# Feed-forward with 512-column products: the whole inner width first, then the down projection by output tile

## The chip, the cores and the metric

The kernel runs on one core of a Trainium2 chip. The metric is the device time of one execution in microseconds (us); smaller is better. The kernel before takes 1467.88 us as a median of three runs.

## The reference, cut to what matters

A network of two blocks works on 256 tokens of width 1024. The first block is two mixing layers with attention (called "even" and "odd" in the kernel). The second has two layers, each a feed-forward, a mixing stage, and another feed-forward; a norm ends it. The change lies in the feed-forward, which therefore runs four times (fa0, fb0, fa1, fb1):

```python
x = x + 0.5 * swiglu(rms_norm(x, norm), w_gate, w_up, w_down)
```

`swiglu(h)` is `(silu(h @ w_gate) * (h @ w_up)) @ w_down`, with an inner width of 2816, all in float32.

## The kernel before, in words

Activations lie with features on the 128 partitions and the 256 tokens along the free axis, so `x` is 8 tiles of 128 x 256. To keep float32 accuracy with the one-pass type float32r, every operand is split in a high part (rounded to float32r) and a low part (what the rounding left). A product of weight tile `w` and activation `h` is then three matmuls (`mm3`, L131 to L133): w-high with h-high, w-high with h-low, w-low with h-high, each with 256 columns, all added in one PSUM tile. The 128 x 128 weight tile is the stationary operand and is loaded anew for every matmul.

Weights come as one stream. `fetch_to` loads pieces of 128 x 1024 (512 KB) on SP's DMA queue, and for each ScalarE casts the high part (`whi`, L117) and VectorE subtracts (`wlo`, L118). There are 4 raw buffers and 5 of `whi` and `wlo`; `weight` asks for the piece 4 places ahead, so a new piece takes the buffers of the piece that TensorE has just left.

The feed-forward before (`ffn`): `scaled` makes high and low parts of `x` times the norm's gain (two separate tiles per feature tile, `hh` and `hl`). The inner width is 22 tiles. For inner tile m, `gate_up` accumulates gate and up in the two halves of one PSUM bank (2 x 8 x 3 = 48 matmuls), and `swish` multiplies by the token's norm factor straight from PSUM (L257, 512 wide), applies silu on ScalarE (L259), multiplies gate and up (L260), and splits the result (L139, L140). `down(m)` then adds this tile's part of all 8 output tiles in 4 PSUM banks (24 matmuls), two inner tiles behind the gate and up products. After the last, L242 adds half of each sum to `x`. The norm's factor comes from `squares`, `rms_sum` (L207), 12 small VectorE instructions (L185 to L191), and `rms_spread` (transposes, L199) in the middle of inner tile 2.

A scheduler of the framework puts each engine's instructions in one fixed order when the program is built; at run time each engine works through its own list and waits where an input is not there.

Of the kernel before, what the change touches and what calls it, by code (L numbers as in the profile page):

```python
# [9 lines left out]
F32 = mybir.dt.float32  # L10
# [3 lines left out]
OP = mybir.AluOpType  # L14
# [37 lines left out]
class Net:  # L52
# [90 lines left out]
    def scaled(self, gain):  # L143

        nc, ring = self.nc, self.ring
        self.h = []
        for k in range(KT):
            x = self.x[k]
            hi = ring.tile([128, S], F32R, tag=f"hh{k}", name=f"hh{k}")
            lo = ring.tile([128, S], F32R, tag=f"hl{k}", name=f"hl{k}")  # L150
            g = self.gain0[:, k:k + 1] if gain == "norm0" else self.v(gain, k)
            nc.scalar.activation(hi, x, AF.Copy, scale=g)
            nc.vector.scalar_tensor_tensor(lo, x, g, hi.bitcast(F32), op0=OP.mult, op1=OP.subtract)
            self.h.append((hi, lo))

    def squares(self):

# [63 lines left out]
    def half_silu(self, out, t):  # L221

        self.nc.scalar.activation(out, t, AF.Tanh)
        self.nc.vector.scalar_tensor_tensor(out, out, 1.0, t, op0=OP.add, op1=OP.mult)

    def ffn(self, tag, gain):
        nc, tc = self.nc, self.tc
        with ExitStack() as c:
            psum = self.banks.using(gu=(2, 0, 1), ss=(3,), acc0=(4,), acc1=(5,), acc2=(6,), acc3=(7,))
            work = c.enter_context(tc.tile_pool(name="fw", bufs=1))  # L230
            self.scaled(gain)
            acc = [psum.tile([128, 2, S], F32, tag=f"acc{i}", name=f"acc{i}") for i in range(4)]
            mid = {}

            def down(m):
                mh, ml = mid.pop(m)
                for i in range(KT):
                    self.mm3(acc[i // 2][:, i % 2], *self.weight((tag, "d", m), i * 128), mh, ml,
                             start=(m == 0 and i % 2 == 0), stop=(m == MT - 1))
                    if m == MT - 1 and i % 2 == 1:  # L240
                        for j in (i - 1, i):
                            nc.vector.scalar_tensor_tensor(self.x[j], acc[i // 2][:, j % 2], 0.5, self.x[j],  # L242
                                                           op0=OP.mult, op1=OP.add)

            def gate_up(m):
                ps = psum.tile([128, 2, S], F32, tag="gu", name="gu")
                if m == 1:
                    self.squares()
                if m == 2:
                    self.rms_sum(psum)  # L250
                self.feature_tiles(ps, (tag, "gu", m), first=m == 0,
                                   mid=(lambda: self.rms_spread(psum)) if m == 2 else None)
                return ps

            def swish(m, ps):
                t = work.tile([128, 2, S], F32, tag="t", name="t", bufs=2)
                nc.vector.tensor_tensor(t, ps, self.rsb, op=OP.mult)  # L257
                g = work.tile([128, S], F32, tag="g", name="g", bufs=2)
                nc.scalar.activation(g, t[:, 0], AF.Silu)  # L259
                nc.vector.tensor_tensor(g, g, t[:, 1], op=OP.mult)  # L260
                mid[m] = self.split(work, g, "m", bufs=4)

            ps = [gate_up(m) for m in range(3)]
            for m in range(3):
                swish(m, ps[m])
            down(0)
            for m in range(3, MT):
                swish(m, gate_up(m))
                down(m - 2)
            down(MT - 2)  # L270
            down(MT - 1)

    def feature_tiles(self, ps, key, first=False, mid=None):

# [61 lines left out]
    def ysplit(self, src_fn, k):  # L336

        nc, ring = self.nc, self.ring
        hi = ring.tile([128, S], F32R, tag=f"hh{k}", name=f"yh{k}")
        lo = ring.tile([128, S], F32R, tag=f"hl{k}", name=f"yl{k}")  # L340
        src = src_fn
        nc.scalar.copy(hi, src)
        nc.vector.tensor_tensor(lo, src, hi.bitcast(F32), op=OP.subtract)
        self.y[k] = (hi, lo)
# [894 lines left out]
    def final(self, gain, out):  # L1239
# [4 lines left out]
        o = [self.ring.tile([128, 4, S], F32, tag="raw", name="o", bufs=RAW) for _ in range(2)]  # L1244
        ps = psum.tile([128, 2], F32, tag="sum", name="sum")
        for k in range(KT):
            t = self.ring.tile([128, S], F32, tag=f"hl{k}", name="t")
# [28 lines left out]
def _cols(w, i, n=128):  # L1276
    return w[:, i * n:(i + 1) * n]
# [7 lines left out]


def _ffn(add, tag, gate, up, down):
    for m in range(MT + 2):
        if m < MT:
            add((tag, "gu", m), _t(_cols(gate, m), _cols(up, m)))  # L1290
        if m >= 2:
            add((tag, "d", m - 2), _n(down[(m - 2) * 128:(m - 1) * 128]))


HEADS = [h for t in range(4) for h in (t, 4 + t)]
# [222 lines left out]
```

## Time and profile before

| | us |
|---|---|
| median of 3 runs (1467.38 to 1471.15) | 1467.88 |
| the profiled execution | 1467.17 |
| its span on the core | 1465.4 |
| TensorE busy with matmuls | 1432.1 (98%) |
| VectorE busy | 1013.0 (69%) |
| ScalarE busy | 739.8 (50%) |
| mean granted TensorE clock | 0.991 of full speed |

The profile shows one execution. PE is TensorE's matmuls, PEld its weight loads, DVE is VectorE, ACT is ScalarE, SP issues the DMAs. Matmuls are pipelined: the duration of one overlaps the next, so what one costs is read from start to start in a timeline, not from its duration. The other 1.8 us of the profiled execution lie outside the span.

### The profile page before, as it was taken

The page shows a single profiled execution, that of the slowest core. Times are in us where ns is not written, and L with a number is a line of the kernel's source. Part 1 is how long each engine was busy: PE and PEld are TensorE (multiplying, and loading weights), DVE is VectorE, ACT ScalarE, POOL GpSimd, SP SyncE. Part 2 cuts the span into 40 slices and gives each one's busy share as a digit, 9 for nine tenths or more (in the row PEclk, how much of TensorE's full clock was granted, in tenths as well). Part 3 has the DMA queues.
Part 4 walks back from the last instruction along what each step waited for, and adds up shares of the span by engine and source line. Part 5 has one row for each costly group of instructions (what it writes and reads, how often), then busy time and mean ns, then how long its engine had stood idle before and what let it go on. Part 6 is the DMA issues. An engine that isn't in the chain of part 4 may idle for free.

```text
span 1465.4 us, 31747 instructions
## 1 busy us (share of the span) xinstructions
PE 1432.1 (98%) x13326; PEld 1370.9 (94%) x13326; DVE 1013.0 (69%) x1804; ACT 739.8 (50%) x1268; POOL 23.9 (2%) x54
## 2 busy tenths in 40 slices
PE   8899989999999999999999999999999999999997
PEld 7699979899999989898999999999998988999997
DVE  7879798886555678657655668556678756765564
ACT  6947555855444474335444445444457324544443
POOL 0000000000000000000000000000000001000000
PEclk9999999999999999999999999999999999999998
DMA  8244534265555534124555555555553213555551
GB/s 297 76 130 132 179 125 144 87 206 177 186 184 184 180 116 129 47 87 122 180 181 182 187 187 173 184 178 187 187 173 116 74 32 101 173 178 183 186 187 44
DMA packets 63600, 222.01 MB, mean 151 GB/s; under 512 B 7744, under 2 KB 9024, under 8 KB 63456
## 3 DMA queue, kind: packets, MB, share of 16 engines
q1 hardware_dynamic: 62928, 219.31, 47.0%
q8 instruction: 104, 1.70, 0.5%
q10 hardware_dynamic: 432, 0.53, 0.1%
q14 instruction: 40, 0.33, 0.1%
q0 software_dynamic: 96, 0.13, 0.0%
HBM read 218.90 MB, written 1.05 MB: 150 GB/s over the span
## 4 chain that ended last, share of the span: by engine, by line
PE 91%; ACT 4%; DVE 3%; issue 1%; POOL 1%; DMA 0%; POOLq 0%; DVEq 0%; ACTq 0%
PE gu L131 11%; PE gu L133 11%; PE gu L132 11%; PE mm L132 6%; PE mm L131 6%; PE mm L133 6%; PE acc L131 6%; PE acc L132 6%; PE acc L133 6%; PE t L975 2%; PE dx L975 1%; PE gram L992 1%; PE gu L282 1%; PE s L370 1%; ACT whi L117 1%
## 5 line engine op out<-in xcount | busy, mean ns | idle before, releaser
L118 DVE TENSOR_TENSOR wlo<-raw,whi 128x1024 fp32r<-128x1024 f32 (+1 forms) x412 | 499.1, 1213 | 209.2 <-ACT whi L117 208.8
L117 ACT CAST whi<-raw 128x1024 fp32r<-128x1024 f32 (+1 forms) x412 | 426.8, 1039 | 416.8 <-PE gu L132 167.4
L131 PE MATMUL gu<-hh,whi 128*128 128x256 f32 x1344 | 380.7, 283 | 0.1
L132 PE MATMUL gu<-hl,whi 128*128 128x256 f32 x1344 | 380.3, 283 | 0.0
L133 PE MATMUL gu<-hh,wlo 128*128 128x256 f32 x1344 | 380.2, 283 | 0.0
L131 PEld LDWEIGHTS gu<-hh,whi 128*128 128x128 f32 x1344 | 257.3, 191 | 0.6 <-issue 0.2
L133 PEld LDWEIGHTS gu<-hh,wlo 128*128 128x128 f32 x1344 | 257.4, 192 | 0.0
L132 PEld LDWEIGHTS gu<-hl,whi 128*128 128x128 f32 x1344 | 257.3, 191 | 0.0
L132 PE MATMUL acc<-ml,whi 128*128 128x256 f32 x704 | 197.6, 281 | 0.0
L133 PE MATMUL acc<-mh,wlo 128*128 128x256 f32 x704 | 197.5, 281 | 0.0
L131 PE MATMUL acc<-mh,whi 128*128 128x256 f32 x704 | 196.9, 282 | 0.1
L131 PE MATMUL mm<-hh,whi 128*128 128x256 f32 x608 | 178.4, 293 | 6.8 <-ACT whi L117 6.5
L132 PE MATMUL mm<-hl,whi 128*128 128x256 f32 x608 | 175.8, 289 | 0.1
L133 PE MATMUL mm<-hh,wlo 128*128 128x256 f32 x608 | 175.6, 289 | 0.0
L132 PEld LDWEIGHTS acc<-ml,whi 128*128 128x128 f32 x704 | 132.7, 189 | 0.0
L131 PEld LDWEIGHTS acc<-mh,whi 128*128 128x128 f32 x704 | 132.0, 189 | 0.7 <-ACT mh L139 0.3
L133 PEld LDWEIGHTS acc<-mh,wlo 128*128 128x128 f32 x704 | 132.5, 188 | 0.0
L131 PEld LDWEIGHTS mm<-hh,whi 128*128 128x128 f32 x608 | 117.1, 193 | 11.3 <-ACT whi L117 6.5
L132 PEld LDWEIGHTS mm<-hl,whi 128*128 128x128 f32 x608 | 117.2, 193 | 2.9 <-issue 1.2
L133 PEld LDWEIGHTS mm<-hh,wlo 128*128 128x128 f32 x608 | 117.0, 192 | 2.2 <-issue 0.9
L257 DVE TENSOR_TENSOR t<-gu,rs 128x512 f32<-128x512 f32 x88 | 60.4, 690 | 54.8 <-PE gu L133 54.8
L139 ACT CAST mh<-g 128x256 fp32r<-128x256 f32 x88 | 35.3, 406 | 100.4 <-DVE g L260 100.4
(396 smaller groups left out, 2210.2 us busy)
## 6 DMA issues: line engine op xcount, KB each, us to landing
raw<-in_stream SPq DMA_DIRECT2D x404, 512.0 KB, 3.5
raw<-in_stream SPq DMA_DIRECT2D x4, 280.0 KB, 2.6
x<-in_x SPq DMA_DIRECT2D x4, 256.0 KB, 5.0
raw<-in_stream SPq DMA_DIRECT2D x4, 256.0 KB, 5.2
lora<-in_lora SPq DMA_DIRECT2D x2, 512.0 KB, 5.1
dec<-in_dec SPq DMA_DIRECT2D x1, 512.0 KB, 5.5
out<-o SPq DMA_DIRECT2D x2, 256.0 KB, 3.0
out<-o ACTq DMA_DIRECT2D x2, 256.0 KB, 2.8
```

Of the source, the lines that this page charges most:

```text
L117: nc.scalar.copy(hi, raw)
L118: nc.vector.tensor_tensor(lo, raw, hi.bitcast(F32), op=OP.subtract)
L131: mm(out, ah, bh, start=start, stop=False, skip_group_check=True)
L132: mm(out, ah, bl, start=False, stop=False, skip_group_check=True)
L133: mm(out, al, bh, start=False, stop=stop, skip_group_check=True)
L139: nc.scalar.copy(hi, src)
L257: nc.vector.tensor_tensor(t, ps, self.rsb, op=OP.mult)
L282: mm(ps[:, u], part, self.h[k][0], start=(i + j == 0), stop=False, skip_group_check=True)
L370: nc.tensor.matmul(ps[:, 0:256], q[p, 128:256], kT[p, :], start=True, stop=True)
L975: nc.tensor.matmul(ps[p, n], lhs(e, p, n), rhs(e, p, n), start=True, stop=True)
L992: nc.tensor.matmul(ps[p, n], bk[p, 4 * u + n, w], ar[p, 4 * u + n], start=True, stop=True)
```

## The change

- `mmw` replaces `mm3` in the feed-forward. High and low part of an activation lie side by side in one tile, and one matmul of 512 columns multiplies w-high with both; its two results go to the two halves of a PSUM bank. A second matmul of 256 columns adds w-low with the high part to the first half. Three matmuls become two; the columns are the same.
- Gate and up now take a bank each, and whoever reads a result must add the two halves: ScalarE copies the second half out of PSUM, VectorE adds the first.
- The whole inner width comes first (22 tiles of gate and up, all results kept in SBUF), then `down` output tile by output tile, 22 products each, each followed by its own copy, add, factor and add to `x`. The norm's factor is multiplied into the gate before silu, and into the output at the end instead of into `up`.
- The weight stream is laid out in that order; the pieces keep their size and number.

```diff
     def scaled(self, gain):
...
-            hi = ring.tile([128, S], F32R, tag=f"hh{k}", name=f"hh{k}")
-            lo = ring.tile([128, S], F32R, tag=f"hl{k}", name=f"hl{k}")
+            t = ring.tile([128, 2, S], F32R, tag=f"h{k}", name=f"h{k}")
+            hi, lo = t[:, 0], t[:, 1]
...
+            self.hw.append(t.rearrange("p a t -> p (a t)"))
...
+    def mmw(self, out, ah, al, b, start, stop):
+
+        mm = self.nc.tensor.matmul
+        mm(out.rearrange("p a t -> p (a t)"), ah, b, start=start, stop=False, skip_group_check=True)
+        mm(out[:, 0], al, b[:, 0:S], start=False, stop=stop, skip_group_check=True)
...
-            psum = self.banks.using(gu=(2, 0, 1), ss=(3,), acc0=(4,), acc1=(5,), acc2=(6,), acc3=(7,))
+            psum = self.banks.using(gu=(0, 1, 2, 3, 4, 5), ss=(6,), dn=(7, 6, 2, 3))
...
             def swish(m, ps):
-                t = work.tile([128, 2, S], F32, tag="t", name="t", bufs=2)
-                nc.vector.tensor_tensor(t, ps, self.rsb, op=OP.mult)
-                g = work.tile([128, S], F32, tag="g", name="g", bufs=2)
-                nc.scalar.activation(g, t[:, 0], AF.Silu)
-                nc.vector.tensor_tensor(g, g, t[:, 1], op=OP.mult)
-                mid[m] = self.split(work, g, "m", bufs=4)
+
+                g = work.tile([128, 2, S], F32, tag="g", name="g", bufs=3)
+                for u in range(2):
+                    nc.scalar.copy(g[:, u], ps[u][:, 1])
+                    nc.vector.tensor_tensor(g[:, u], ps[u][:, 0], g[:, u], op=OP.add)
+                    if u == 0:
+                        nc.vector.tensor_tensor(g[:, 0], g[:, 0], self.rs, op=OP.mult)
+                        nc.scalar.activation(g[:, 0], g[:, 0], AF.Silu)
+                nc.vector.tensor_tensor(g[:, 0], g[:, 0], g[:, 1], op=OP.mult)
+                t = work.tile([128, 2, S], F32R, tag=f"m{m}", name="m")
+                nc.scalar.copy(t[:, 0], g[:, 0])
+                nc.vector.tensor_tensor(t[:, 1], g[:, 0], t[:, 0].bitcast(F32), op=OP.subtract)
+                mid.append(t.rearrange("p a t -> p (a t)"))
...
-            down(0)
             for m in range(3, MT):
                 swish(m, gate_up(m))
-                down(m - 2)
-            down(MT - 2)
-            down(MT - 1)
+            for i in range(KT):
+                acc = psum.tile([128, 2, S], F32, tag="dn", name="acc")
+                for m in range(MT):
+                    self.mmw(acc, *self.weight((tag, "d"), (i * MT + m) * 128), mid[m], m == 0, m == MT - 1)
+                t = work.tile([128, S], F32, tag="t", name="t", bufs=2)
+                nc.scalar.copy(t, acc[:, 1])
+                nc.vector.tensor_tensor(t, acc[:, 0], t, op=OP.add)
+                nc.vector.tensor_tensor(t, t, self.rs2[:, 0], op=OP.mult)
+                nc.vector.tensor_tensor(self.x[i], self.x[i], t, op=OP.add)
...
+    for m in range(MT):
+        add((tag, "gu", m), _t(_cols(gate, m), _cols(up, m)))
+    add((tag, "d"), down.reshape(MT, 128, KT, 128).transpose(1, 2, 0, 3).reshape(128, -1))
```

TensorE, second feed-forward, where down and gate/up products meet. Before they alternate every 48 and 24 rows (`hh`, `hl`: parts of `x`; `mh`, `ml`: parts of an inner tile):

```order
L133 MATMUL acc3_11091<-mh_11326,wlo_11285 128x256
L131 MATMUL gu_11469<-hh0_11056,whi_11341 128x256
L132 MATMUL gu_11469<-hl0_11057,whi_11341 128x256
L133 MATMUL gu_11469<-hh0_11056,wlo_11342 128x256
L131 MATMUL gu_11469<-hh1_11060,whi_11341 128x256
L132 MATMUL gu_11469<-hl1_11061,whi_11341 128x256
```

With the change the last gate/up product is followed by the first of output tile 0 (`m` is an inner tile with both parts):

```order
L230 MATMUL gu_11400<-h6_10158,whi_11311 128x512
L231 MATMUL gu_11400<-h6_10158,wlo_11312 128x256
L230 MATMUL gu_11400<-h7_10161,whi_11311 128x512
L231 MATMUL gu_11400<-h7_10161,wlo_11312 128x256
L230 MATMUL acc_11456<-m_10347,whi_11346 128x512
L231 MATMUL acc_11456<-m_10347,wlo_11347 128x256
L230 MATMUL acc_11456<-m_10358,whi_11346 128x512
L231 MATMUL acc_11456<-m_10358,wlo_11347 128x256
```

Each group of three rows is now two, and the down rows stand together behind all 22 inner tiles.

VectorE, one inner tile of the same feed-forward. Before:

```order
L257 TENSOR_TENSOR t_11831<-gu_11770,rs_11279 128x512
L118 TENSOR_TENSOR wlo_11843<-raw_11840,whi_11842 128x1024
L260 TENSOR_TENSOR g_11833<-g_11833,t_11831 128x256
L140 TENSOR_TENSOR ml_11837<-g_11833,mh_11836 128x256
L118 TENSOR_TENSOR wlo_11874<-raw_11871,whi_11873 128x1024
L118 TENSOR_TENSOR wlo_11904<-raw_11901,whi_11903 128x1024
```

With the change, VectorE and then ScalarE, the same inner tile (L262 copies the second half, L263 adds the first):

```order
L263 TENSOR_TENSOR g_11331<-gu_11285,g_11331 128x256
L265 TENSOR_TENSOR g_11331<-g_11331,rs_10314 128x256
L118 TENSOR_TENSOR wlo_11347<-raw_11344,whi_11346 128x1024
L263 TENSOR_TENSOR g_11331<-gu_11286,g_11331 128x256
L267 TENSOR_TENSOR g_11331<-g_11331 128x256
L118 TENSOR_TENSOR wlo_11369<-raw_11366,whi_11368 128x1024
L270 TENSOR_TENSOR m_11339<-g_11331,m_11339 128x256
```

```order
L262 COPY g_11331<-gu_11285 128x256
L117 CAST whi_11346<-raw_11344 128x1024
L266 ACTIVATE g_11331<-g_11331 128x256
L262 COPY g_11331<-gu_11286 128x256
L117 CAST whi_11368<-raw_11366 128x1024
L269 CAST m_11339<-g_11331 128x256
```

Per inner tile there are now two weight pieces instead of three, and five small VectorE rows instead of one of 512 columns and two of 256; ScalarE has four small rows instead of two, with a weight cast behind each of the two copies.

TensorE, first mixing stage, up to the spread that waits for ScalarE's `wide`. Before, the head sums (L912) stand 16 rows ahead of it:

```order
L131 MATMUL mm_7184<-hh2_6427,whi_6704 128x256
L132 MATMUL mm_7184<-hl2_6428,whi_6704 128x256
L133 MATMUL mm_7184<-hh2_6427,wlo_6705 128x256
L131 MATMUL mm_7184<-hh3_6431,whi_6704 128x256
L132 MATMUL mm_7184<-hl3_6432,whi_6704 128x256
L133 MATMUL mm_7184<-hh3_6431,wlo_6705 128x256
L131 MATMUL mm_7184<-hh4_6435,whi_6704 128x256
L903 MATMUL spread_6815<-ident_74,wide_6813 128x128 x4
```

With the change they stand 12 rows ahead of it:

```order
L131 MATMUL mm_6710<-h0_5953,whi_6230 128x256
L132 MATMUL mm_6710<-h0_5953,whi_6230 128x256
L133 MATMUL mm_6710<-h0_5953,wlo_6231 128x256
L131 MATMUL mm_6710<-h1_5956,whi_6230 128x256
L132 MATMUL mm_6710<-h1_5956,whi_6230 128x256
L133 MATMUL mm_6710<-h1_5956,wlo_6231 128x256
L131 MATMUL mm_6710<-h2_5959,whi_6230 128x256
L918 MATMUL spread_6341<-ident_74,wide_6339 128x128 x4
```

The scheduler moved the spread six rows forward, and the sums two; the second mixing stage has the same shift.

## Rows read from the trace of the kernel before

**Rows 1.** The page: TensorE busy, and the data moved in 40 slices.
```profile
PE 1432.1 (98%) x13326; PEld 1370.9 (94%) x13326; DVE 1013.0 (69%) x1804; ACT 739.8 (50%) x1268; POOL 23.9 (2%) x54
...
GB/s 297 76 130 132 179 125 144 87 206 177 186 184 184 180 116 129 47 87 122 180 181 182 187 187 173 184 178 187 187 173 116 74 32 101 173 178 183 186 187 44
```

**Rows 2.** Windows of the four feed-forward stretches; the columns stand in the first line.
```profile
core 0: us, PE busy (x) PEld busy (x) DVE busy (x) ACT busy (x) POOL busy (x), PEclk, DMA share, GB/s
317.70:508.90 191.20, 191.07 (x1595) 190.57 (x1595) 119.50 (x159) 87.70 (x119) 0.00 (x0) 1.00 0.58 182
...
sum 764.90, PE 764.33 PEld 762.32 DVE 474.70 ACT 347.55 POOL 0.00; mean PE 191.08 PEld 190.58 DVE 118.68 ACT 86.89 POOL 0.00
```

**Rows 3.** Timeline of TensorE, inner products of one tile, 35 in a row (start, duration).
```profile
336.84 0.28 PE L132 MATMUL gu<-hl,whi 128*128 128x256 f32 x1
...
340.91 0.28 PE L133 MATMUL gu<-hh,wlo 128*128 128x256 f32 x1
```

**Rows 4.** Timeline of TensorE, down products, 48 in a row.
```profile
500.40 0.28 PE L131 MATMUL acc<-mh,whi 128*128 128x256 f32 x1
...
505.99 0.28 PE L133 MATMUL acc<-mh,wlo 128*128 128x256 f32 x1
```

**Rows 5.** Timeline of TensorE, products of 512 columns, 44 in a row.
```profile
162.02 0.40 PE L332 MATMUL mm<-wlo,hh 128*128 128x512 f32 x1
...
171.79 0.39 PE L333 MATMUL mm<-whi,hl 128*128 128x512 f32 x1
```

**Rows 6.** Groups by line, and the rows of two tiles: one instruction on VectorE and ScalarE.
```profile
L118 DVE TENSOR_TENSOR wlo<-raw,whi 128x1024 fp32r<-128x1024 f32 x66 | 80.7, 1225 | 45.1 <-ACT whi L117 45.1
L117 ACT CAST whi<-raw 128x1024 fp32r<-128x1024 f32 x66 | 68.9, 1047 | 74.4 <-PE gu L132 44.1 <-issue 28.8 <-PE acc L132 1.3
...
L260 DVE TENSOR_TENSOR g<-g,t 128x256 f32<-128x256 f32 x22 | 9.2, 420 | 0.7 <-ACT g L259 0.7
...
L411 ACT COPY pt<-t x16: 357/374/379, 113.6 to 294.5; 128x256 f32<-128x256 f32 x16
...
L242 DVE SCALAR_TENSOR_TENSOR x<-acc,x x32: 410/414/425, 507.0 to 1452.5; 128x256 f32<-128x256 f32 x32
```

**Rows 7.** Timeline of ScalarE and VectorE inside one inner tile before.
```profile
501.48 0.41 ACT L259 ACTIVATE g<-t 128x256 f32<-128x256 f32 x1
...
502.75 0.42 DVE L260 TENSOR_TENSOR g<-g,t 128x256 f32<-128x256 f32 x1
...
503.20 0.41 ACT L139 CAST mh<-g 128x256 fp32r<-128x256 f32 x1 [1.31 <-DVE g L260]
...
503.64 0.42 DVE L140 TENSOR_TENSOR ml<-g,mh 128x256 fp32r<-128x256 f32 x1 [0.47 <-ACT mh L139]
```

**Rows 8.** Timeline: reciprocal root of the mean square, and the transpose that waits for it.
```profile
330.31 0.16 DVE L185 TENSOR_SCALAR ra<-ss 128x2 f32<-128x2 f32 x1 [1.48 <-PE ss L207]
...
333.45 0.28 PE L131 MATMUL gu<-hh,whi 128*128 128x256 f32 x1
333.50 0.16 DVE L191 SCALAR_TENSOR_TENSOR ry<-rt,ry 128x2 f32<-128x2 f32 x1
333.80 0.40 PE L199 MATMUL spread<-ident,ry 128*128 128x128 f32 x2
```

**Rows 9.** Timeline of TensorE, last product before the first feed-forward and its first.
```profile
317.52 0.28 PE L133 MATMUL mm<-yh,wlo 128*128 128x256 f32 x1
317.72 0.38 PE L282 MATMUL gu<-hh,whi 128*128 128x256 f32 x1
```

**Rows 10.** Timeline in the mixing stage: head sums, and the spread that waits for them.
```profile
541.25 1.05 PE L912 MATMUL sums<-e,kkq 128*128 128x2 f32 x8 [0.52 <-ACT kkq L941]
...
544.67 0.62 ACT L899 COPY wide<-rr 128x512 f32<-128x512 f32 x1 [2.04 <-POOL rr L175]
...
545.34 0.66 PE L903 MATMUL spread<-ident,wide 128*128 128x128 f32 x4 [1.02 <-ACT wide L899]
```

**Rows 11.** Timeline of TensorE, final norm.
```profile
1451.99 3.78 PE L1250 MATMUL sum<-ones,t 128*128 128x1 f32 x32
```

More of the change, by code (lines that the diff above doesn't have):

```diff
@@ L145, in scaled @@
         nc, ring = self.nc, self.ring
-        self.h = []
+        self.h, self.hw = [], []
         for k in range(KT):
             x = self.x[k]
-            hi = ring.tile([128, S], F32R, tag=f"hh{k}", name=f"hh{k}")
-            lo = ring.tile([128, S], F32R, tag=f"hl{k}", name=f"hl{k}")
+            t = ring.tile([128, 2, S], F32R, tag=f"h{k}", name=f"h{k}")
+            hi, lo = t[:, 0], t[:, 1]
             g = self.gain0[:, k:k + 1] if gain == "norm0" else self.v(gain, k)
@@ L228, in ffn @@
         with ExitStack() as c:
-            psum = self.banks.using(gu=(2, 0, 1), ss=(3,), acc0=(4,), acc1=(5,), acc2=(6,), acc3=(7,))
+            psum = self.banks.using(gu=(0, 1, 2, 3, 4, 5), ss=(6,), dn=(7, 6, 2, 3))
             work = c.enter_context(tc.tile_pool(name="fw", bufs=1))
             self.scaled(gain)
[L232 to L243, printed above, removed]
+            mid = []
             def gate_up(m):
-                ps = psum.tile([128, 2, S], F32, tag="gu", name="gu")
+                ps = [psum.tile([128, 2, S], F32, tag="gu", name="gu") for _ in range(2)]
                 if m == 1:
@@ L250, in gate_up @@
                     self.rms_sum(psum)
-                self.feature_tiles(ps, (tag, "gu", m), first=m == 0,
-                                   mid=(lambda: self.rms_spread(psum)) if m == 2 else None)
+                its = [(u, k) for u in range(2) for k in range(KT)]
+                if m == 0:
+                    its = [(u, k) for k in range(KT) for u in range(2)]
+                for i, (u, k) in enumerate(its):
+                    if m == 2 and i == KT:
+                        self.rms_spread(psum)
+                    self.mmw(ps[u], *self.weight((tag, "gu", m), (u * KT + k) * 128), self.hw[k], k == 0, k == KT - 1)
                 return ps
             def swish(m, ps):
-                t = work.tile([128, 2, S], F32, tag="t", name="t", bufs=2)
-                nc.vector.tensor_tensor(t, ps, self.rsb, op=OP.mult)
-                g = work.tile([128, S], F32, tag="g", name="g", bufs=2)
-                nc.scalar.activation(g, t[:, 0], AF.Silu)
-                nc.vector.tensor_tensor(g, g, t[:, 1], op=OP.mult)
-                mid[m] = self.split(work, g, "m", bufs=4)
+                g = work.tile([128, 2, S], F32, tag="g", name="g", bufs=3)
[10 more added lines that the diff above has]
+                mid.append(t.rearrange("p a t -> p (a t)"))
             ps = [gate_up(m) for m in range(3)]
@@ L338, in ysplit @@
         nc, ring = self.nc, self.ring
-        hi = ring.tile([128, S], F32R, tag=f"hh{k}", name=f"yh{k}")
-        lo = ring.tile([128, S], F32R, tag=f"hl{k}", name=f"yl{k}")
+        t = ring.tile([128, 2, S], F32R, tag=f"h{k}", name=f"yy{k}")
+        hi, lo = t[:, 0], t[:, 1]
         src = src_fn
@@ L1246, in final @@
         for k in range(KT):
-            t = self.ring.tile([128, S], F32, tag=f"hl{k}", name="t")
+            t = self.ring.tile([128, 2, S], F32, tag=f"h{k}", name="t")[:, 0]
             nc.scalar.activation(t, self.x[k], AF.Square)
@@ L1287, in _ffn @@
 def _ffn(add, tag, gate, up, down):
[L1288 to L1292, printed above, removed]
+    for m in range(MT):
+        add((tag, "gu", m), _t(_cols(gate, m), _cols(up, m)))
+    add((tag, "d"), down.reshape(MT, 128, KT, 128).transpose(1, 2, 0, 3).reshape(128, -1))
 HEADS = [h for t in range(4) for h in (t, 4 + t)]
```

## The prediction

> **What bounds the kernel now.** I read the page first. TensorE is busy for 1432.1 of 1465.4 us [rows 1], so the first question is what the feed-forward takes of that, and whether TensorE ever waits in it. The windows answer both: the four feed-forward stretches make 764.90 us together, about 191.2 each, and TensorE is busy for 764.33 of them, at a granted clock of 1.00 [rows 2]. VectorE is busy for 474.70 us there and ScalarE for 347.55, so neither is the bound [rows 2]. Half of the kernel is thus one dense row of matmuls, and a change is worth what it does to the distance from one start to the next.
>
> That distance is read from the timeline, since durations overlap. 35 inner products start within 340.91 - 336.84 = 4.07 us, which is 34 steps of 119.7 ns [rows 3]. 48 down products start within 5.59 us, 47 steps of 118.9 ns [rows 4]. At the full clock of 2.4 GHz, 256 columns take 106.7 ns, so each matmul pays about 13 ns beyond its columns. The question of this change is whether those 13 ns belong to a matmul or to its columns. The kernel has one place with 512 columns, in the attention layer "odd": 44 matmuls of the same type, each with a new stationary tile, start within 9.77 us, 43 steps of 227.2 ns [rows 5]. Their columns take 213.3 ns; 13.9 ns are left. So the surcharge is paid once per matmul and hardly grows with the columns.
>
> **The change, part by part.**
>
> *Three matmuls become two.* A group of three costs 3 x 119.7 = 359.1 ns in gate and up [rows 3] and 3 x 118.9 = 356.7 ns in down [rows 4]. The pair costs 227.2 [rows 5] + 119.7 = 346.9 ns. Gate and up have 4 x 22 x 16 = 1408 groups: 1408 x 12.2 ns = 17.2 us. Down has 4 x 22 x 8 = 704: 704 x 9.8 ns = 6.9 us. Together **-24.1 us**. All of it lies on the path, because TensorE is the bound there. The one assumption is that a 512-column matmul among 256-column ones costs what it costs among its like. The bounds are below, among the rivals.
>
> *More work per inner tile on ScalarE and VectorE.* An inner tile now lasts 16 x 346.9 ns = 5.55 us; before, its 72 matmuls took 8.6. VectorE has two weight subtractions of 1.225 us and five operations of 0.42 us [rows 6]: 4.55 us, or 82%. ScalarE has two weight casts of 1.05, two copies from PSUM of 0.37 [rows 6], silu and cast of 0.41 each [rows 7]: 3.66 us, or 66%. Both fit under TensorE. A handover between the two engines costs about 0.03 us (cast ends at 503.61, subtraction starts at 503.64) [rows 7]. They work with slack: three inner tiles fit in the six PSUM banks, and weights are asked for four pieces ahead, 4 x 8 x 346.9 ns = 11 us. The rows of the new order put a weight cast or subtraction into most gaps between the small steps, so the two engines alternate rather than stand still. I cost it at 0. If that cover goes, it becomes the rival on the other side.
>
> *The down projection apart.* An output tile takes 22 x 346.9 ns = 7.63 us; VectorE does 2.75 weight pieces, three small operations and a low part in it: 5.05 us. Its first product needs inner tile 0, and inner tile 21 only 7.3 us after the phase has begun, later than the last swish needs. Cost 0.
>
> *Weight transfers.* A piece of 512 KB is used up in 8 x 346.9 ns = 2.78 us, 189 GB/s. The stretches move 182 now [rows 2] and other slices up to 206 and 297 [rows 1]. Cost 0.
>
> *The norm's factor.* The chain of small VectorE instructions runs from 330.31 to 333.66, one weight subtraction in it, and the transpose starts 0.35 us after the matmul ahead of it, some 0.23 late [rows 8]. The new order puts an addition of 0.41 [rows 6] into the chain. It leaves 21 rows (11 of 512 columns, 10 of 256: 3.70 us) between norm sums and transpose; before it was 28 rows (3.35 us). So 0.07 us more per feed-forward: **+0.3 us**. If a second weight subtraction falls into the chain it is 1.2 each; if none is late, -0.9 in all.
>
> *Entering a feed-forward.* Three of the four follow an output projection. There the gap is 0.20 us from start to start now, 0.08 over the step [rows 9], because the first 32 products need only high parts. Now the first product needs high and low part of feature tile 0. In the order of the first one VectorE first has two additions, a weight subtraction and three low parts to do, 0.82 + 1.22 + 1.26 = 3.3 us [rows 6], after a matmul whose result comes 0.28 us later; TensorE has 24 products (2.87 us) to cover it. That leaves 0.7 us, some 0.6 more than now: **+1.6 us** for three (0 to 3.6). The fourth follows a feed-forward, whose first seven output tiles are long finished: its last one goes through copy, three VectorE operations, and both parts, 0.37 + 3 x 0.42 + 0.83 = 2.5 us, while 14 pairs (4.9 us) come first. Cost 0.
>
> *After a feed-forward.* The mixing stage has 34 products of 120 ns ahead of the first that needs the last feature tile, 4.1 us against those 2.5. In the final norm 28 of the 32 sums (3.3 of 3.78 us [rows 11]) cover copy, three operations and a square. Cost 0 for both.
>
> *Mixing stages.* The scheduler moves the head sums two rows and the spread six rows forward, in both. The spread already waits for ScalarE's `wide`, which starts 3.4 us after the sums, with TensorE idle for 1.02 us [rows 10]. Four rows less cover are 4 x 0.12 = 0.5 us each: **+1.0 us** (-1 to +3, since ScalarE's and VectorE's lists move too).
>
> Sum: 1467.2 (the profiled execution) - 24.1 + 0.3 + 1.6 + 1.0 = 1446.0. The median of the runs is 0.7 us above the profiled execution, and I predict for that: **1446.5 us**, 1.5% faster.
>
> **The rivals.**
>
> *The surcharge belongs to the columns.* Then 512 columns among 256-column matmuls cost 2 x 119.7 ns, and the change gains nothing: 1446.5 + 24.1 = 1470.6. For it: no pair of this kind stands in the trace, and the 512-column rows have weights as the moving operand and activations as the stationary one. Against it: the 227.2 ns [rows 5] are the same type, with a new stationary tile each time. Chance 0.06. The Trainium skill ("TensorE: Matmul & The Clock Gate", Back-to-back issue gap) speaks against most of the gain too: it gives the distance of isolated matmuls as their columns at 2.4 GHz plus 2.5 ns. By that rule each matmul removed saves 2.5 ns, an estimate of 2112 x 2.5 = 5.3 us in all. The trace does not agree here: with a weight load for each matmul it shows 13 to 14 ns instead of 2.5, at 256 and at 512 columns.
>
> *The second matmul of a pair loses its surcharge,* because its weight load has the double time under the 512 columns. The pair then costs 227.2 + 106.7 ns, 2112 x 13.0 = 27.5 us less: 1419. Against it: the 512-column rows have such loads under 512 columns as well, and still pay 13.9 ns. Chance 0.05.
>
> *The swish chain becomes the bound: slower.* Each of ScalarE and VectorE works through a fixed list, and the steps of an inner tile go back and forth between them. If they ran one behind the other, an inner tile would take nine small steps of 0.37 to 0.42 (3.65), nine handovers (0.3) and two weight subtractions with nothing beside them (2.45): 6.4 us against TensorE's 5.55. The three tiles in PSUM postpone that but don't mend it. Over 19 tiles and four feed-forwards it costs 76 x 0.85 = 65 us: 1511. It decides from a period of 5.55 + 21.2 / 76 = 5.83 us on. For it: VectorE at 82%. Against it: the copy, silu and second copy of a tile stand beside weight subtractions in the order, and VectorE's own sum is a full microsecond below. Chance 0.06.
>
> **How the numbers follow.** The forecast has 0.80, the three rivals 0.17, and 0.03 is for nothing of these. The forecast's own bounds (norm factor -0.9 to +4.6, entries -1.6 to +2.0, mixing stages -2 to +2, the pair's distance by 1 ns or 2.1 us) give some 8 us either way, not all at once: **1438 to 1455**. A measurement of this kernel can tell about 0.3%, 4.4 us. Faster by more: the forecast, the larger gain and part of the rest, 0.87. Within 0.3%: the column rival, 0.06. Slower: the chain and what is left, 0.07.
>
> **What would show it.** In the timeline of the changed kernel the 512-column matmul and the next should start 347 ns after one another pairwise, and a feed-forward stretch should last about 185.5 us with TensorE without gaps. Pairs of 359 ns show the first rival, of 334 the second. A gate/up phase with waits of TensorE on `gu` banks or `whi`, and inner tiles 6 us apart, shows the third. The weight part is wrong if TensorE waits for `whi` with ScalarE waiting for a DMA, the entry if the first `gu` product starts at once or more than a microsecond late, the mixing term if `spread` waits much more or less than 1.5 us.

## The result, and the profile after

The changed kernel takes 1444.16 us as a median of four runs (1443.4 to 1445.3), the kernel before 1467.63 us beside it. The ratio is 0.9841, with an interval of 0.9829 to 0.9853: 1.6% faster. The profiled execution took 1444.65 us, its span 1442.9 us, at the same mean granted clock of 0.991.

The page after, TensorE's busy time and the data moved in 40 slices, answers to [rows 1]:

```profile
PE 1411.0 (98%) x11214; PEld 1259.9 (87%) x11214; DVE 1076.2 (75%) x2044; ACT 797.3 (55%) x1476; POOL 23.6 (2%) x54
...
GB/s 292 87 132 118 174 149 148 62 205 190 191 189 185 187 128 118 50 78 126 183 182 188 190 188 177 190 191 190 189 176 118 75 31 103 164 188 190 190 188 45
```

TensorE is 98% busy as before, with 2112 matmuls fewer. The transfers kept up at up to 191 GB/s.

The windows of the feed-forward stretches, from the start of the first matmul to the start of the last (fb0 and fa1 are one stretch), answer to [rows 2], whose first line names the columns:

```profile
318.48:503.53 185.05, 185.05 (x1065) 162.76 (x1066) 139.18 (x228) 104.91 (x178) 0.00 (x0) 1.00 0.59 188
687.40:1059.88 372.48, 372.48 (x2133) 325.01 (x2132) 276.68 (x451) 208.00 (x352) 0.00 (x0) 1.00 0.58 187
1243.72:1428.88 185.16, 185.16 (x1068) 162.73 (x1066) 130.10 (x214) 101.46 (x177) 0.00 (x0) 1.00 0.51 168
sum 742.69, PE 742.69 PEld 650.50 DVE 545.95 ACT 414.37 POOL 0.00; mean PE 247.56 PEld 216.84 DVE 181.98 ACT 138.12 POOL 0.00
```

Cut in the same way, the stretches before took 764.5 us (191.11, 382.48, 190.91). So 21.8 of the 22.5 us by which the span fell lie in the feed-forward, and TensorE still has no idle time there. The rest nearly cancels: +0.8 until the first feed-forward, -1.4 and -0.6 in the two mixing stages between, +0.5 behind the last.

The timeline of TensorE after, in order of time: the entry of the first feed-forward (answers to [rows 9]), the norm's transpose ([rows 8]), inner products of fa0 ([rows 3]), down products ([rows 4]), the mixing stage's sums and spread ([rows 10]), inner products of fb0, and the final norm ([rows 11]):

```profile
317.57 0.28 PE L133 MATMUL mm<-yy,wlo 128*128 128x256 f32 x1
318.48 0.50 PE L230 MATMUL gu<-h,whi 128*128 128x512 f32 x1 [0.63 <-DVE h L153]
...
334.06 0.39 PE L230 MATMUL gu<-h,whi 128*128 128x512 f32 x1
334.38 0.40 PE L200 MATMUL spread<-ident,ry 128*128 128x128 f32 x2
...
399.92 0.39 PE L230 MATMUL gu<-h,whi 128*128 128x512 f32 x1
400.15 0.28 PE L231 MATMUL gu<-h,wlo 128*128 128x256 f32 x1
...
402.35 0.39 PE L230 MATMUL gu<-h,whi 128*128 128x512 f32 x1
...
469.94 0.39 PE L230 MATMUL acc<-m,whi 128*128 128x512 f32 x1
...
472.75 0.40 PE L230 MATMUL acc<-m,whi 128*128 128x512 f32 x1
...
535.47 1.05 PE L927 MATMUL sums<-e,kkq 128*128 128x2 f32 x8 [0.20 <-ACT kkq L956]
...
539.19 0.66 PE L918 MATMUL spread<-ident,wide 128*128 128x128 f32 x4 [1.13 <-ACT wide L914]
...
759.94 0.40 PE L230 MATMUL gu<-h,whi 128*128 128x512 f32 x1
...
762.77 0.40 PE L230 MATMUL gu<-h,whi 128*128 128x512 f32 x1
...
1428.99 4.52 PE L1265 MATMUL sum<-ones,t 128*128 128x1 f32 x32
```

Seven pairs in fa0 take 402.35 - 399.92 = 2.43 us, 347 ns each: 230 for the wide matmul, 117 for the narrow one. Eight down pairs take 2.81 us, 351 ns each. But eight pairs of the same kind in fb0 take 2.83 us, 354 ns each. The whole inner part of fb0 goes at that pace: it takes 125.4 us, where the other three take 123.3 to 123.4. Its pairs are not all alike: the distances, to the nanosecond of the trace, repeat as 349, 350, 361 from beginning to end, while in fa0 nearly every pair behind the norm's transposes takes 346 or 347. The four down parts take 61.7 each.

One difference is not the change's. Before, one window in the first mixing stage had half the clock for a while. The windows of 10 us in the same place of the stage, first before and then after:

```profile
640.00:650.00 10.00, 9.61 (x63) 9.04 (x63) 5.73 (x11) 4.59 (x7) 3.28 (x2) 0.83 0.18 54
```

```profile
633.00:643.00 10.00, 9.60 (x70) 8.67 (x69) 5.80 (x12) 5.13 (x8) 3.27 (x2) 1.00 0.16 47
```

The mean of 0.83 can cost (1 - 0.83) x 10 = 1.7 us at most. What it did cost is seen beside the second mixing stage, which has no drop: 185.2 and 184.4 us before, 183.9 and 183.8 after. So 0.8 of the 1.4 us by which the first became shorter is the drop's, and 0.6 went in both stages. Such drops come and go between executions of one kernel (in the ten runs of one experiment below the mean clock went from 0.987 to 0.991), and some of the differences of 1 to 3 us below are theirs.

### The profile page after: what moved, and what is told of

Read it like the earlier page. It is cut to its first block, busy times and chain, and to the rows that moved or that the text cites. A ratio compares the mean times of both kernels' runs of the same rounds, so it can differ in the third digit from the quotient of the medians.

```text
span 1442.9 us, 28160 instructions
## 1 busy us (share of the span) xinstructions
PE 1411.0 (98%) x11214; PEld 1259.9 (87%) x11214; DVE 1076.2 (75%) x2044; ACT 797.3 (55%) x1476; POOL 23.6 (2%) x54
## 3 DMA queue, kind: packets, MB, share of 16 engines
q8 instruction: 88, 1.44, 0.4%
## 4 chain that ended last, share of the span: by engine, by line
PE 91%; ACT 4%; DVE 3%; issue 1%; POOL 1%; DMA 0%; POOLq 0%; SPq 0%; DVEq 0%; ACTq 0%
PE gu L230 23%; PE gu L231 12%; PE acc L230 11%; PE mm L131 6%; PE mm L132 6%; PE mm L133 6%; PE acc L231 6%; PE t L990 2%; PE dx L990 1%; ACT whi L117 1%; PE gram L1007 1%; PE s L385 1%; PE mm L333 1%; PE mm L332 1%; PE mm L334 1%
## 5 line engine op out<-in xcount | busy, mean ns | idle before, releaser
L230 PE MATMUL gu<-h,whi 128*128 128x512 f32 x1408 | 491.9, 394 | 0.6 <-DVE h L153 0.6
L231 PE MATMUL gu<-h,wlo 128*128 128x256 f32 x1408 | 393.8, 280 | 0.0
L230 PEld LDWEIGHTS gu<-h,whi 128*128 128x128 f32 x1408 | 263.8, 187 | 61.4 <-DVE h L153 0.8
L231 PEld LDWEIGHTS gu<-h,wlo 128*128 128x128 f32 x1408 | 265.6, 189 | 0.1
L230 PE MATMUL acc<-m,whi 128*128 128x512 f32 x704 | 247.3, 393 | 0.0
L231 PE MATMUL acc<-m,wlo 128*128 128x256 f32 x704 | 199.1, 283 | 0.0
L131 PE MATMUL mm<-h,whi 128*128 128x256 f32 x608 | 178.7, 294 | 6.5 <-ACT whi L117 6.2
L132 PE MATMUL mm<-h,whi 128*128 128x256 f32 x608 | 176.0, 289 | 0.1
L133 PE MATMUL mm<-h,wlo 128*128 128x256 f32 x608 | 175.0, 288 | 0.0
L131 PEld LDWEIGHTS mm<-h,whi 128*128 128x128 f32 x608 | 117.1, 193 | 11.3 <-ACT whi L117 6.5
L132 PEld LDWEIGHTS mm<-h,whi 128*128 128x128 f32 x608 | 117.1, 193 | 2.8 <-issue 1.2
L131 PE MATMUL mm<-yy,whi 128*128 128x256 f32 x256 | 72.9, 288 | 0.4 <-DVE zt L839 0.4
L132 PE MATMUL mm<-yy,whi 128*128 128x256 f32 x256 | 73.0, 286 | 0.0
L263 DVE TENSOR_TENSOR g<-gu,g 128x256 f32<-128x256 f32 x176 | 73.0, 418 | 0.0
L262 ACT COPY g<-gu 128x256 f32<-128x256 f32 x176 | 63.0, 361 | 0.0
```

The lines of the kernel that those rows point to most:

```text
L131: mm(out, ah, bh, start=start, stop=False, skip_group_check=True)
L132: mm(out, ah, bl, start=False, stop=False, skip_group_check=True)
L133: mm(out, al, bh, start=False, stop=stop, skip_group_check=True)
L230: mm(out.rearrange("p a t -> p (a t)"), ah, b, start=start, stop=False, skip_group_check=True)
L231: mm(out[:, 0], al, b[:, 0:S], start=False, stop=stop, skip_group_check=True)
L262: nc.scalar.copy(g[:, u], ps[u][:, 1])
```

## The experiments

Two questions had to be separated: whether the gain is the merged matmul or the new order, and what a merged pair really costs. Then came the rivals: whether ScalarE and VectorE were near to being the bound, and what a matmul pays beside its columns.

### The new order with three matmuls

```diff
-        mm(out.rearrange("p a t -> p (a t)"), ah, b, start=start, stop=False, ...)
+        mm(out[:, 0], ah, b[:, 0:S], start=start, stop=False, ...)
+        mm(out[:, 1], ah, b[:, S:2 * S], start=False, stop=False, ...)
```

> The changed kernel with one difference: every 512-column matmul of the feed-forward is split again into two of 256 columns (w-high with the high part, w-high with the low part), into the same two halves of the same bank. Order of the work, banks, adds and weight stream stay. Theory (a surcharge of some 13 ns per matmul): groups are back at 357 to 360 ns, a feed-forward stretch back at 190.5 to 191.5 us, the time at 1444.2 + 24 = 1468 us (1465 to 1471). Rival (the gain comes from the order, whole inner width first, or from the norm's factor being moved): the time stays at 1444 to 1449 us.

It took 1466.16 us (10 runs), ratio to before 0.9992 (0.9983 to 1.0002), inside the theory's range. Its timeline, four groups of three apart:

```profile
399.73 0.28 PE L230 MATMUL gu<-h,whi 128*128 128x256 f32 x1
...
401.17 0.28 PE L230 MATMUL gu<-h,whi 128*128 128x256 f32 x1
```

A group costs 1.44 / 4 = 360 ns, as before. The order, the banks and the longer chain on ScalarE and VectorE are all in this kernel, and by the medians nothing is gained or lost that a measurement can tell. Five of its ten runs had a mean clock of 0.992 and took 1464.2 to 1465.8 us; the 13 runs of the kernel before beside them, at 0.991 to 0.993, took 1466.3 to 1468.0. At the same clock the order thus brings some 2 us, which the five runs at 0.988 to 0.990 lose again. All the rest of the gain needs the merge.

### Three matmuls in the down projection alone

```diff
-                    self.mmw(acc, *self.weight((tag, "d"), (i * MT + m) * 128), mid[m], m == 0, m == MT - 1)
+                    self.mm3w(acc, *self.weight((tag, "d"), (i * MT + m) * 128), mid[m], m == 0, m == MT - 1)
```

> The changed kernel with the split into three matmuls only in the down projection; gate and up stay merged. Theory with the prediction's sizes: 704 x 9.8 ns = 6.9 us come back, 1451 us. Theory with the pair's distance as the trace of the changed kernel shows it in down (351 ns instead of 347): 704 x 5.7 ns = 4.0 us come back, 1448 us. Rival (merging does nothing in down): 1444 us.

It took 1446.93 us (4 runs), ratio 0.9863 (0.9848 to 0.9878): 2.8 us above the changed kernel's median, with intervals that overlap. That is nearest to the second theory, but the times alone don't rule out the rival. Its down products, five groups apart:

```profile
469.86 0.28 PE L230 MATMUL acc<-m,whi 128*128 128x256 f32 x1
...
471.64 0.28 PE L230 MATMUL acc<-m,whi 128*128 128x256 f32 x1
```

A group costs 1.78 / 5 = 356 ns, the pair 351. That is 704 x 5 = 3.5 us for the merge in the down projection, so merging does something there, and most of the gain is left to gate and up.

### The merge in gate and up with the old order, twice

The first of these kernels keeps the interleaved order, the stream and the down projection of the kernel before, and merges gate and up alone. As in the changed kernel, the norm's factor for up is multiplied in at the end of a feed-forward, so an output tile takes two VectorE operations there.

```diff
-            for i in range(KT):
-                acc = psum.tile([128, 2, S], F32, tag="dn", name="acc")
...
+                swish(m, combine(gate_up(m)))
+                down(m - 2)
...
+                            nc.vector.tensor_tensor(t, acc[i // 2][:, j % 2], self.rs2[:, 0], op=OP.mult)
+                            nc.vector.tensor_tensor(self.x[j], self.x[j], t, op=OP.add)
```

> Merged matmuls in gate and up alone, in the order and with the weight stream of the kernel before: down follows two inner tiles behind, in four accumulator banks, with three matmuls; gate and up share the four other banks, so that only two inner tiles fit in PSUM. Theory (the merge is the gain, the order is not needed for speed): 1408 x 11 ns = 15.5 us below the kernel before, 1452 us (1449 to 1455). Rival (the new order was needed to make room): TensorE waits for gu banks each inner tile, and the time is 1460 us or more.

It took 1476.82 us (4 runs), ratio 1.0062 (1.0047 to 1.0077): slower than before. The time lies in the range of the rival, but not for its reason, since TensorE never waited for a bank inside a feed-forward. The timeline of TensorE at the seam between fb0 and fa1, then that of VectorE:

```profile
885.91 0.28 PE L133 MATMUL acc<-mh,wlo 128*128 128x256 f32 x1
890.85 0.77 PE L230 MATMUL gu<-h,whi 128*128 128x512 f32 x1 [4.67 <-DVE h L153]
```

```profile
885.90 0.75 DVE L253 TENSOR_TENSOR t<-acc,rs 128x256 f32<-128x256 f32 x2
886.57 0.75 DVE L254 TENSOR_TENSOR x<-x,t 128x256 f32<-128x256 f32 x2
...
890.23 0.47 DVE L153 SCALAR_TENSOR_TENSOR h<-x,vec,h 128x256 fp32r<-128x256 f32 x1
```

In the old order all eight output tiles end within 3 us. Their 16 operations stand in a row ahead of the first low part, and the first wide product needs that low part. TensorE waits 4.7 us, and afterwards its clock is at half for some time (the wide matmul lasts 0.77 instead of 0.39; the granted clock is the last number but two in this row):

```profile
890.00:895.00 5.00, 4.15 (x13) 3.60 (x14) 5.00 (x12) 1.42 (x4) 0.00 (x0) 0.50 0.00 0
```

This kernel had twice the VectorE work of the kernel before at the seam. The second version multiplies the factor into gate and up in the middle (one operation of 512 columns) and ends with one operation per output tile, as before:

```diff
-                nc.vector.tensor_tensor(g[:, 0], g[:, 0], self.rs, op=OP.mult)
+                nc.vector.tensor_tensor(g, g, self.rsb, op=OP.mult)
...
+                            nc.vector.scalar_tensor_tensor(self.x[j], acc[i // 2][:, j % 2], 0.5, self.x[j], op0=OP.mult, op1=OP.add)
```

> Wide pairs in gate and up only, old interleaved order, as in the experiment of that name, but the end of a feed-forward takes one VectorE operation per output tile as before (the factor is multiplied into gate and up in the middle of an inner tile, one operation of 512 columns). Theory (what the old order lost were its 16 VectorE operations in a row at the seam, 0.33 us each, and what stood behind them): eight fewer take 2.7 us off each seam, the wait of 4.7 us at the seam of the second and third feed-forward falls to about 2, and the mixing stages come back near 184 to 186 us: 1456 to 1464 us. Rival (alternating wide pairs and groups of three is slow in itself, in the mixing stages too): 1470 us or more.

It took 1465.21 us (10 runs), ratio 0.9984 (0.9974 to 0.9993), 1 us above the theory's range and 5 below the rival's. The seam on TensorE, then on VectorE:

```profile
886.24 0.28 PE L133 MATMUL acc<-mh,wlo 128*128 128x256 f32 x1
888.77 0.47 PE L230 MATMUL gu<-h,whi 128*128 128x512 f32 x1 [2.25 <-DVE h L153]
```

```profile
885.50 2.73 DVE L252 SCALAR_TENSOR_TENSOR x<-acc,x 128x256 f32<-128x256 f32 x8
```

The wait fell by 2.4 us to 2.25, near the 2.7 of eight operations of 0.33 us. So the work at the end of a feed-forward is where the first version lost much of its time: 11.6 us separate the two medians, of which this seam is 2.4 and the half clock behind it at most 3.4. The mixing stages did not come back to 184 to 186 us in this profile: they took 189.2 and 186.9, where the changed kernel takes 183.9 and 183.8. Drops of the clock are at most 5.1 and 1.7 of that, as in this window:

```profile
640.00:650.00 10.00, 9.24 (x45) 8.00 (x44) 4.47 (x10) 2.63 (x4) 3.27 (x2) 0.66 0.01 2
```

Waits are another part: TensorE waits 5.6 us in all for `wide`, in the changed kernel 3.1. The profiled run, at 1468.3, is the slowest of its ten.

So the order alone brings 2 us at most, and the merge in gate and up with the old order brings 2 us. With the new order the same merge brings 19 (1466.16 to 1446.93). Of the 17 us between, 8 are the pair's pace: the mean distance is 353.7 ns over all 1408 pairs here and 348.1 in the kernel with three matmuls in down, 1408 x 5.6 = 7.9 us. The old order breaks the pairs up into short rows between down products, and 74 of its 82 rows repeat the slower pattern 349, 350, 361. The seam is 2.3, and the first feed-forward starts 1.2 us later than in the changed kernel. The rest was not taken apart; the mixing stages hold much of it, and the mean clock was 0.987 to 0.991 in these ten runs against 0.992 to 0.993 in the four with three matmuls in down.

### More work for VectorE

Two kernels add multiplications to each inner tile whose results nobody reads; the first two of them, the second four.

```diff
+                d = work.tile([128, S], F32, tag="dummy", name="dummy", bufs=2)
+                for _ in range(4):
+                    nc.vector.tensor_tensor(d, g[:, 0], g[:, 1], op=OP.mult)
```

> The changed kernel with two more multiplications of 128 x 256 on VectorE per inner tile, whose result nobody reads. Theory (VectorE has a sum of work per inner tile, and only above TensorE's 5.55 us does it count): 4.55 + 0.84 = 5.39 us, so nothing changes, 1444 to 1447 us. Rival (the chain that goes back and forth between ScalarE and VectorE is what nearly bounds): each addition lengthens the period past 5.55 us, 1460 us or more.

> As the run before, with four more. Theory: 4.55 + 1.68 = 6.23 us by durations, above 5.55; VectorE is the bound in gate and up, 76 tiles x 0.68 = 52 us more, 1496 us; as back-to-back operations overlap by some 0.05 us each, 0.45 us less per tile, the lower end is 1460 us. Rival (VectorE has far more room than the sum of durations says): 1444 to 1447 us.

They took 1446.5 and 1447.64 us (one run each): the first in its theory's range, the second 0.6 us above its rival's. The same 95 us of fa0, first with four more operations, then in the changed kernel:

```profile
345.00:440.00 95.00, 95.00 (x550) 83.77 (x549) 94.37 (x196) 57.68 (x104) 0.00 (x0) 1.00 0.60 193
```

```profile
345.00:440.00 95.00, 95.00 (x549) 83.75 (x548) 74.16 (x121) 55.93 (x103) 0.00 (x0) 1.00 0.60 193
```

VectorE is busy for 94.37 of 95 us and TensorE loses nothing. The 1496 us that I expected for four is far off, and the timeline of VectorE in this kernel shows why:

```profile
400.23 0.42 DVE L263 TENSOR_TENSOR g<-gu,g 128x256 f32<-128x256 f32 x1
400.56 0.41 DVE L274 TENSOR_TENSOR dummy<-g 128x256 f32<-128x256 f32 x1
400.90 0.42 DVE L265 TENSOR_TENSOR g<-g,rs 128x256 f32<-128x256 f32 x1
...
401.90 1.22 DVE L118 TENSOR_TENSOR wlo<-raw,whi 128x1024 fp32r<-128x1024 f32 x1
403.04 0.42 DVE L267 TENSOR_TENSOR g<-g 128x256 f32<-128x256 f32 x1
```

Each small operation lasts 0.42 us, but the next starts after 0.335; the weight subtraction lasts 1.22, and the next starts after 1.14. This holds where the next doesn't read what the one just before it wrote. Where it does, as L265 behind L263 in the changed kernel, it starts 0.46 us after it, and other work can go in between:

```profile
402.95 0.42 DVE L263 TENSOR_TENSOR g<-gu,g 128x256 f32<-128x256 f32 x1
403.41 0.42 DVE L265 TENSOR_TENSOR g<-g,rs 128x256 f32<-128x256 f32 x1
```

Nine small ones and two subtractions are 9 x 0.335 + 2 x 1.14 = 5.3 us, still under TensorE's 5.55. The few microseconds that the two kernels took more come from elsewhere. The second has two inner parts at the slower pace instead of one (374.5 us in the middle stretch), 2.2 us. The first has one, as the changed kernel has (fa0 at 187.3 us instead of fb0), and its feed-forwards take the same 742.8 us; it lost 1.1 us in the second mixing stage, where its clock dropped, and 0.5 before the first feed-forward.

### The narrow matmul first

```diff
-        mm(out.rearrange("p a t -> p (a t)"), ah, b, start=start, stop=False, ...)
-        mm(out[:, 0], al, b[:, 0:S], start=False, stop=stop, ...)
+        mm(out[:, 0], al, b[:, 0:S], start=start, stop=False, ...)
+        mm(out.rearrange("p a t -> p (a t)"), ah, b, start=False, stop=stop, ...)
```

> The changed kernel with the two matmuls of a pair in the other order: w-low (256 columns) first, w-high (512 columns) second. Theory (each matmul pays a fixed surcharge, whatever stands before it): pairs of 347 to 351 ns, 1444 us (1442 to 1447). Rival (the 117 ns of the 256-column matmul come from standing behind 512 columns of the same activations, or the steady distance depends on the sequence): pairs of 353 ns or more, or of 344 or less; 1455 us or more, or 1438 us or less.

It took 1448.22 us (4 runs), ratio 0.9867 (0.9853 to 0.9882), between the theory's range and the rival's. Seven pairs of fa0:

```profile
399.75 0.40 PE L231 MATMUL gu<-h,whi 128*128 128x512 f32 x1
...
402.23 0.40 PE L231 MATMUL gu<-h,whi 128*128 128x512 f32 x1
```

A pair costs 2.48 / 7 = 354 ns, in three of the four inner parts (125.4 to 125.5 us); one ran at 123.2. So both orders know both paces, and the order within a pair does not decide between them. The slower pace costs 2 us per feed-forward, and two more parts at it make the 4 us to the changed kernel.

### The narrow matmul cut in two

```diff
-        mm(out[:, 0], al, b[:, 0:S], start=False, stop=stop, skip_group_check=True)
+        for c in (0, 128):
+            mm(out[:, 0, c:c + 128], al, b[:, c:c + 128], start=False, stop=stop and c > 0, skip_group_check=True)
```

> The changed kernel with the 256-column matmul of each pair split into two of 128 columns with the same weights: 2112 matmuls more, the same columns. Theory A (a fixed surcharge of 13 ns per matmul, at any width): 2112 x 13 = 27.5 us more, 1472 us. Theory B (a matmul with its own weight load starts at most every 115 to 120 ns, and the 256-column distance is that bound rather than columns plus surcharge): each part takes about 117 ns, 2112 x 117 = 247 us more, 1690 us. Theory C (loads of 128 columns bound at 107 ns): 2112 x 97 = 205 us more, 1649 us.

It took 1670.55 us (one run), 226 us more than the changed kernel, or 107 ns for each of 2112 groups. Its timeline of matmuls, then of weight loads:

```profile
399.58 0.45 PE L230 MATMUL gu<-h,whi 128*128 128x512 f32 x1
399.87 0.33 PE L232 MATMUL gu<-h,wlo 128*128 128x128 f32 x2
400.04 0.45 PE L230 MATMUL gu<-h,whi 128*128 128x512 f32 x1
```

```profile
399.87 0.19 PEld L232 LDWEIGHTS gu<-h,wlo 128*128 128x128 f32 x1
399.98 0.19 PEld L230 LDWEIGHTS gu<-h,whi 128*128 128x128 f32 x1
400.09 0.43 PEld L232 LDWEIGHTS gu<-h,wlo 128*128 128x128 f32 x2
```

A fixed surcharge of 13 ns per matmul would have given 1472; one more matmul costs eight times that. Theories B and C, both of a bound by the weight load, lie 20 us above and 22 below. The weight loads start 0.11 us after one another where they are densest, and a matmul of 128 columns has only 53 ns of columns to lie under. That a matmul narrower than the load pays for the load fits this, and so does the final norm, here from the kernel with the new order and three matmuls:

```profile
1450.16 3.63 PE L1266 MATMUL sum<-ones,t 128*128 128x1 f32 x32
```

Its 32 matmuls have one column each and a weight tile of their own, and start 112 ns after one another at a granted clock of 1.00. The Trainium skill ("TensorE: Matmul & The Clock Gate", LDWEIGHTS) gives a weight load as its columns at 1.2 GHz, 107 ns for 128; the trace agrees with 108 to 112 ns from one load to the next where they are densest.

### The same merge in the output projections

```diff
-                        self.mm3(ps[:, u], *self.weight((tag, "out", half, b), ((p * 2 + u) * 4 + k) * 128),
-                                 *self.y[half * 4 + k], start=(u == 0 and k == 0), stop=(k == 3))
+                        self.mmw(ps, *self.weight((tag, "out", half, b), ((p * 2 + u) * 4 + k) * 128),
+                                 self.y[half * 4 + k], k == 0, k == 3)
...
+                    for a in range(2):
+                        nc.vector.tensor_tensor(self.x[i], ps[:, a], self.x[i], op=OP.add)
```

> The changed kernel with the merged pair in the four output projections as well: 4 x 64 groups of three become pairs, each result in a bank of its own, and VectorE adds both halves to x one after the other. Theory: 256 x (359 - 347 to 353) = 1.5 to 3.1 us less on TensorE, less up to 0.8 us for one more addition ahead of three feed-forwards: 1441.5 to 1443.5 us. Rival (the doubled additions, 0.42 us each, 64 more, delay the following feed-forward or stage): 1445 us or more.

It took 1449.03 us (4 runs), ratio 0.9881 (0.9865 to 0.9898): 5 us slower than the changed kernel and in the rival's range. The entry of its first feed-forward, then two of TensorE's waits in the whole execution (us, times, longest):

```profile
320.52 0.28 PE L231 MATMUL mm<-yy,wlo 128*128 128x256 f32 x1
322.37 0.50 PE L230 MATMUL gu<-h,whi 128*128 128x512 f32 x1 [1.57 <-DVE h L153]
```

```profile
PE gu L230 <- DVE h L153: 4.9, 3, 1.7
PE mm L230 <- DVE x L373: 2.8, 3, 1.6
```

The gap is 1.85 us, where the changed kernel has 0.92 (317.57 to 318.48). The other two entries after a projection have 1.9 and 2.0 us, where the changed kernel has 0.12, a plain step. Inside the projections TensorE waits another 2.8 us until VectorE has added a result and its bank is free (L373). A sum of only four products is too short to hide two additions per output tile on VectorE: the pairs save less than these lose.

## Why the prediction was right, and where its sizes were off

I predicted 1446.5 us (1438 to 1455) and the kernel took 1444.2. The cause was the one named: TensorE's dense row of matmuls is the bound, and a merged pair costs less than three. That the time came within 2 us is in part luck. The feed-forwards fell by 21.8 us where the terms made 24.1 - 0.3 = 23.8, and all the rest fell by 0.7 where the terms made it rise by 2.6; the two misses nearly cancel.

**The pairs** were mis-sized, at -24.1 us. The kernel with the new order and three matmuls has stretches of 190.93, 381.27 and 190.57, together 762.8 us; against it the pairs save 762.8 - 742.7 = 20.1 us. The down term of 6.9 rested on 346.9 ns, the sum of two steps from different places of the kernel. Measured are 351 against 356 in that kernel, 704 x 5.0 = 3.5 us, half of it. That leaves 16.6 for gate and up, where I had 17.2: fb0 went at 354 ns, and with fb0 at the faster pace it would have been 18.6. "A 512-column matmul among 256-column ones costs what it costs among its like" held to 3 ns at the faster pace, where the sum of 347 came out because the wide one took 230 instead of 227.2 and the narrow one 117 instead of 119.7. In fb0 the wide one takes 233 to 241 and the narrow one 113 to 120, so there it held to 14 ns only.

**The order inside the feed-forward**, costed at 0, brought the other 1.7 us of the 21.8 in that one profile. The medians can't tell 1 us from none (1466.16 against 1467.24); the runs at the same clock show some 2.

**The norm's factor** gave back some 0.8 us in all instead of costing 0.3. The transpose starts 0.32 us after a wide matmul that takes 0.23, so it is 0.09 late instead of the 0.23 of [rows 8]; the four are 0.03 to 0.09 late now and were 0.23 to 0.35. The row from the last norm sum to the transpose grew by 0.22 us (3.99 against 3.77), not by the addition's 0.41.

**Entries** cost +0.7 in all, instead of +1.6. The first was as worked out (0.92 against 0.20 [rows 9], +0.7). The two after the mixing stages are a plain step of 0.12 us, as before: I took the first one's order for all three, and the 0.6 worked out for each makes 1.8, not the 1.6 of the sum.

**Mixing stages** gave back 0.6 us each instead of costing 0.5. The wait for `wide` grew by 0.11 us (1.13 against 1.02 [rows 10]), not 0.5, and the wait for the sums fell from 0.52 to 0.20. I counted the rows on TensorE and held ScalarE's list still, but it moved along with them. The other 0.8 us in the first are the clock drop, which is chance.

**After the feed-forward** the final norm took 4.52 instead of 3.78 us [rows 11]. That makes the +0.5 at the end, and it is not the change's. The last output tile's chain of copy, three operations and square is through at 1431.4 us, before TensorE needs it. But the clock falls to half there, a little earlier in the sums than before:

```profile
1429.00:1431.50 2.50, 2.50 (x26) 2.50 (x24) 1.28 (x3) 0.89 (x3) 0.00 (x0) 1.00 0.00 0
1431.50:1433.50 2.00, 2.00 (x11) 1.93 (x10) 0.00 (x0) 0.29 (x1) 0.00 (x0) 0.50 0.00 0
```

The sums start 112 ns after one another at 1.00 and 213 at 0.50. The kernel with the new order and three matmuls has the same chain, and its sums take 3.63 us. So the cost of 0 was right.

**The rivals.** The pairs' 347 to 354 ns rule out both a pair without gain (359) and one without the second surcharge (334). The swish chain was never near to being the bound. I had VectorE at 82% of an inner tile, from durations. Its busy share is 74.16 / 95 = 78%, and by start to start, where no operation waits for the one before it, it is 5 x 0.335 + 2 x 1.14 = 3.95 us, 71%. Four more operations per inner tile cost TensorE nothing.

The reading that "the surcharge is paid once per matmul" holds from 256 columns on, where the prediction used it. It fails at 128, where it is off by a factor of eight. That could be read from [rows 11] already: 32 matmuls of one column there take 3.78 us, 0.12 us each. And the prediction took the order of the work for indifferent, apart from its ends. With groups of three it nearly is; with pairs, the old order gives most of the gain away.

## What to carry to other kernels

Read what a matmul costs from start to start in its own neighbourhood; merging matmuls that share the stationary operand saves what each pays beyond its columns. Count what the merge makes others do: each result has to be added from two halves, which a sum of 22 products hides and one of 4 does not, and which stands ahead of the next layer if all sums end together. For an engine that seems nearly full, take distances from start to start, since durations overlap there too.

## What the runs showed of the hardware that was not expected

- The same dense row of pairs runs at different steady paces: 347 ns in three inner parts and 354 in fb0 of one execution, at a granted clock of 1.00 and with no wait in the trace; 351 in the down products. Each pace is a repeating pattern: 346 and 347 ns (in fa1 343 and 350 in turn), or 349, 350, 361, or 353, 346, 354 in down. Which part runs at which pace differs from kernel to kernel (narrow matmul first: three of four at 354; the merge in the output projections: none). In all 24 gate/up parts of six kernels (the changed one and five of the experiments) the pattern that follows the norm's transposes in inner tile 2 stays for the 309 or 310 pairs up to the end of the part: 17 times at a mean of 346.7 ns, 7 times at 353.3. Why one or the other starts there was not found; it is worth 2 us per feed-forward.
- VectorE starts an operation of 0.42 us 0.335 us after the one before it, 0.46 if it reads that one's result. A sum of durations makes a row of independent operations a quarter too long.
- Cutting a matmul of 256 columns into two of 128, each with its own weights, costs 107 ns more, not 13. Matmuls of one column with their own weights start 112 ns after one another at a granted clock of 1.00, and 213 at 0.50.
